# Five modulation pieces put into the state space layer, its preparation reordered in layer 0, x loaded from the scalar queue

## The chip, the cores and the metric

The kernel runs on one core of a Trainium2 chip. The metric is the device time of one execution in microseconds (us). A core has engines that each work through an order of their own: PE (TensorE, the matmuls), DVE (VectorE), ACT (ScalarE), POOL (GpSimd) and SP (SyncE, which here only issues transfers). They wait for each other through semaphores.

## What is computed

The reference takes 256 positions of width 1024 through two blocks. The first has four layers; layer i has a mixer (attention, spatial gating, state space, attention) and a conv-gated feed-forward net (FFN), each behind an RMS norm and with a residual. The second block is modulated: 48 vectors are made from a condition vector by one large product, and scale, shift and gate its norms and residuals. Cut to what the change touches:

```python
def s5_layer(xn, w_in, lam_re, lam_im, log_dt, b_re, b_im, c_re, c_im, d_skip, w_glu):
    u = xn @ w_in
    dt = exp(log_dt); mag = exp(dt * lr)
    ar, ai = mag * cos(dt * li), mag * sin(dt * li)      # the layer's sines
    ...                                                  # bbar from ar, ai, b
    x = associative_scan(a, bbar u)                      # along the 256 positions
    y = c_re x.re - c_im x.im + d_skip * u
    a, g = split(gelu(y) @ w_glu)
    return a * sigmoid(g)

mod   = silu(c)     @ w_mod + b_mod                      # 1024 x 6144, for the second block
mod_c = silu(c_ctx) @ w_mod + b_mod
lb    = cumsum(softmax(lb_tab))[layer]                   # lower bounds of the second block's gates
```

## The kernel before

**Weights.** Everything is fp32 in two parts: each half of a weight tile (128 x 1024) gets a rounded copy `wh` on ACT (L347) and a residual `wl` on DVE (L356), and a product is three matmuls (L488 to L490). `Stream` loads tiles of 1 MB in the order of a plan, through SP's queue, into three raw buffers. The next load is issued when the second half of a tile has been split, or, for a tile that is not split, when its matmuls are done with it.

**Order of work.** The program is written as one sequence; each engine gets its instructions in that order. `tick` counts triple matmuls; `after(n, fn)` puts fn's instructions n ticks later, and `spread` does so for a list of steps with gaps. So numbers in tables (`S5`, `PREP`, the gaps in `s5_prep`) set where steps stand.

**Modulation pieces.** The product with `w_mod` is cut into 24 pieces (`mod_units`). A piece is a unit (16 matmuls at L1447 with 32 columns of stationary data, straight from an unsplit weight tile), a copy `mpart` of its 128 x 256 result on ACT (L1450), and a rest (4 small matmuls at L1455, then two ACT operations at L1460). The step of piece n issues the rest of piece n - 1 and then unit n. The first `S5[1]` = 16 pieces are done in the state space layer (called m2), all of them from its third channel tile (kt = 2) on; the other eight stand in the FFN behind it (f2), one for each of its steps j = 1 to 8.

**State space layer** (`s5`, L1244). Four projections psu2.0 to psu2.3 give u. Each is scaled on DVE (`s5_t`) and copied into the layout of u (`s5_u`, L1339). For each of eight channel tiles kt: `vmm` (tile s5v, L1268), `scan` (six operations on DVE, L1283 to L1285), `scan2` (the recurrence itself, L1293), `back` (L1299 to L1302, tile s5_x), `ymm` (tile s5y, L1310 and L1316) and a gelu on ACT (L1323). scan(kt + 1) stands behind ymm(kt).

**Preparation of that layer.** `s5_prep` issues it in layer 0: p0 to p5 make the coefficients on 128 x 32 tiles (p3 has the exponential and the sines on ACT, L1079, with a load of the sine table and one of the table in use before), then placements of B and C. `place_c` and `lower_bounds` (one small exponential on ACT, `lb_e`, L1483) stood at the end of layer 0's attention.

**Layer 0's attention.** psv, psq, psk are projections, v, q0, qh/ql, k0, kh/kl their evictions; z0.kt are the scores of a pair of heads; ze0, zh0, zl0 the softplus chain; its parts zh0 and zl0 go back to PE for the cumulative sums, which are added into z0.kt.

**Start.** SP issues the vectors, the two halves of x around the halves of the first weight tile, then the rest. ACT squares x for the norm (tile `nsq`, one buffer) and DVE adds the squares up.

Of the kernel before, what the change touches and what calls it, by code (L numbers as in the profile page):

```python
# [9 lines left out]
F32 = mybir.dt.float32  # L10
# [6 lines left out]
P = 128  # L17
L = 256
# [36 lines left out]
PREP = (33, 7)  # L55
MODU = 48
X2 = (16, 56, 69, 11, 106, 29, 18, 31)
LAT = (8, 9, 23, 24, 19, 14)
# [47 lines left out]
LATE = ((), (1, 2))  # L106


S5 = (5, 16, 1, 1, 1, 14, 0, 0, 0, 0)


_VEC = [
# [293 lines left out]
class Kern:  # L406
# [113 lines left out]
    def setup(self, pp):  # L520
# [4 lines left out]
        self.xT = self.apool.tile([P, KT, L], F32, name="xT")  # L525
        load = lambda o, i: nc.sync.dma_start(out=o, in_=i)
        load(self.cols[:, :P], ins["vecs"][:, :P])
        half = lambda q: load(self.xT[:, 4 * q:4 * q + 4, :], ins["x"][:, 4 * q:4 * q + 4, :])
        half(0)
        self.W = Stream(self, ins["weights"], lambda: half(1))  # L530
        self.W._load()
# [63 lines left out]
    def norm_square(self, pr, late=()):  # L595
        nc = self.nc
        x = self.xT[:, 2 * pr:2 * pr + 2, :]
        if pr == 0:
            nc.scalar.activation(self.acc, x, AF.Square)
        else:  # L600
            sq = self.pp.tile([P, 2, L], F32, tag="nsq", bufs=1, name=f"sq_{self.nname}_{pr}")
            nc.scalar.activation(sq, x, AF.Square)
            self.add_later(pr, self.acc, sq, late)

# [442 lines left out]
    def s5_prep(self, sp):  # L1047
# [74 lines left out]
        def p5():  # L1122
# [5 lines left out]
            tt(V, t1, am, lim, ALU.mult)  # L1128
            tt(V, t0, t0, t1, ALU.subtract)
            tt(V, cim, t0, den, ALU.mult)  # L1130
        for p, gap in ((p0, 4), (p1, 4), (p2, 4), (p3, 26), (p4, PREP[1]), (p5, PREP[1])):
            step(p, gap)
        b3 = lambda q: q.unsqueeze(2).to_broadcast([P, 32, 16])
        v3 = lambda q: q.rearrange("p (a b) -> p a b", a=32)
# [14 lines left out]
        def place_c():  # L1149
            for q in range(2):  # L1150
                for g in range(2):
                    act(C[:, 2 + q, :, 16 * g:16 * g + 16], v3(Cc[:, q, :]), AF.Copy,
                        scale=sgn[:, 2 * q + g:2 * q + g + 1])
        step(place_c, 0)
        def place(tp, q, e):
            if e == 0:
                st[q] = tp.tile([P, 32, 2, 2, 16], F32, tag="s5e", name=f"s5_E{q}")
# [26 lines left out]
                    V.tensor_copy(K0[o + 32:o + 64, :, 1, :], di[o + 32:o + 64])  # L1184
        def late(tp):

            h = {}
            for q in range(2):
                j = 4 * q + 1
                h[j, "a"] = [lambda q=q: place(tp, q, 0)]  # L1190
                h[j, "g"] = [lambda q=q: place(tp, q, 1)]
                for g in range(3):
                    h[j + 1, "agd"[g]] = [lambda q=q, g=g: trans(q, g)]
                h[j + 2, "a"] = [lambda q=q: trans(q, 3)]
                h[j + 2, "g"] = [lambda q=q: k0(tp, q)]
            return h
# [1060 lines left out]
    def run(self):  # L2257
# [6 lines left out]
        for i in range(DEPTH):  # L2264
# [3 lines left out]
            if m == 2:  # L2268
                with self.phase(f"p_m{i}") as pp:
                    self.fillers = self.mod_units()  # L2270
                    self.s5(i, pp)
                s5.pop().close()
                s5.pop().close()
                pp = pf.enter_context(self.phase(f"p_f{i}"))
                self.s5_glu(i, nx, pp)
                hooks = {}
            else:
                if i == 0:
                    s5.append(ExitStack())
                    self.table = "natural_log_exp_and_others"  # L2280
                    steps, late = self.s5_prep(s5[0].enter_context(self.phase("p_s50", psum=False)))
                    self.spread(PREP[0], [(fn, min(g, PREP[1]) if n > 5 else g) for n, (fn, g) in enumerate(steps)] + [(self.lower_bounds, 0)])
                if i == 3:
                    cp = pc.enter_context(self.phase("p_ctx", psum=False))
                with self.phase(f"p_m{i}") as pp:
                    (self.attention, self.sgu)[m](i, nx, pp)
                if i == 1:
                    s5.append(ExitStack())
                    sp = s5[1].enter_context(self.phase("p_s51", psum=False))
                pp = pf.enter_context(self.phase(f"p_f{i}"))  # L2290
                hooks = late(pp) if i == 0 else self.s5_tables(sp) if i == 1 else {}
                if i == 1:
                    hooks.setdefault((9, "a"), []).append(self.mod_inputs)
# [92 lines left out]
```

## Time and profile before

| | us |
|---|---|
| median of 3 runs | 1621.68 (1620.92 to 1625.38) |
| profiled execution, its own time | 1621.46 |
| its span | 1619.7 |
| PE busy | 1584.7 (98%) |
| DVE busy | 1257.2 (78%) |
| ACT busy | 994.4 (61%) |
| chain that ended last | PE 84%, DVE 8%, ACT 4% |

The profile is of one execution. Its mean granted clock is 0.993 of full speed. Busy shares are averages over stages with different limits; the waits of single engines, with what ended them, and busy time by stretch tell more. Times within the profile count from the start of the span.

### The profile page before, as it was taken

Reading aid. Unit: us, or ns where it says so; the run is one execution under the profiler, and the core shown is the slowest. Engines: PE = TensorE matmul, PEld = TensorE weight load, DVE = VectorE, ACT = ScalarE, POOL = GpSimd, SP = SyncE. Lnnn points to the kernel's source line nnn. Section 1 sums busy time; section 2 is a strip of 40 time slices with the busy share of each in tenths; the row PEclk is TensorE's granted clock in tenths of the full one; section 3 lists DMA queues with packets and bytes.
Section 4 is the critical chain, followed back from the end, with each engine's and each line's share of the span. In section 5 each row is a group of like instructions: output and inputs, shape, how many; then the busy total and the mean of one; then the engine's idle time right before and its main releaser. Section 6 shows DMA issues by size and latency. Waiting matters only on the chain.

```text
span 1619.7 us, 33776 instructions
## 1 busy us (share of the span) xinstructions
PE 1584.7 (98%) x14370; PEld 1533.2 (95%) x14370; DVE 1257.2 (78%) x1897; ACT 994.4 (61%) x1487; POOL 42.8 (3%) x121
## 2 busy tenths in 40 slices
PE   9899999999999989999999999999999999999997
PEld 8889999999999987799999999999999998899997
DVE  6878877778999889878777765898886697786554
ACT  6776666566778653455556677766566563465443
POOL 0000000010000000000000100000003000000000
PEclk9999999999999999999999999999999999999999
DMA  8424554555455525856666432555545521246551
GB/s 309 139 95 172 194 187 179 200 191 186 170 199 216 195 105 209 321 204 233 233 234 227 187 134 105 209 192 199 197 155 215 204 94 53 104 147 230 187 205 53
DMA packets 42918, 294.27 MB, mean 182 GB/s; under 512 B 4944, under 2 KB 6224, under 8 KB 8336
## 3 DMA queue, kind: packets, MB, share of 16 engines
q1 hardware_dynamic: 41984, 289.04, 49.3%
q0 software_dynamic: 784, 3.08, 0.5%
q8 instruction: 112, 1.84, 0.4%
q14 instruction: 38, 0.31, 0.1%
HBM read 291.06 MB, written 1.05 MB: 180 GB/s over the span
## 4 chain that ended last, share of the span: by engine, by line
PE 84%; DVE 8%; ACT 4%; DMA 1%; issue 1%; POOL 0%; SPq 0%; DVEq 0%; ACTq 0%; POOLq 0%
DVE wl L356 2%; DMA raw<-in_weights_dram 1%; PE mod L1447 1%; PE fb L488 1%; PE fb L490 1%; PE fb L489 1%; PE gug L490 1%; PE gug L488 1%; PE gug L489 1%; ACT wh L347 1%; PE gua L488 1%; PE gua L490 1%; PE gua L489 1%; PE s5y L1316 1%; PE mod L1455 1%
## 5 line engine op out<-in xcount | busy, mean ns | idle before, releaser
L356 DVE TENSOR_TENSOR wl<-raw,wh 128x1024 fp32r<-128x1024 f32 (+1 forms) x496 | 594.2, 1214 | 112.5 <-ACT wh L347 29.1
L347 ACT ACTIVATE wh<-raw 128x1024 fp32r<-128x1024 f32 (+1 forms) x496 | 511.2, 1049 | 199.1 <-DMA raw<-in_weights_dram 42.0
L488 PE MATMUL fb<-gph,wh 128*128 128x256 f32 x176 | 49.0, 278 | 0.2 <-DVE gy L2160 0.2
L490 PE MATMUL fb<-gph,wl 128*128 128x256 f32 x176 | 48.7, 277 | 0.0
L489 PE MATMUL fb<-gpl,wh 128*128 128x256 f32 x176 | 48.6, 276 | 0.0
L490 PE MATMUL gug<-xh_f,wl 128*128 128x256 f32 x144 | 39.9, 277 | 1.2 <-DVE wl L356 1.2
L488 PE MATMUL gug<-xh_f,wh 128*128 128x256 f32 x144 | 39.8, 276 | 0.0
L489 PE MATMUL gug<-xl_f,wh 128*128 128x256 f32 x144 | 39.8, 276 | 0.0
L490 PE MATMUL gua<-xh_f,wl 128*128 128x256 f32 x144 | 39.8, 276 | 0.0
L489 PE MATMUL gua<-xl_f,wh 128*128 128x256 f32 x144 | 39.8, 276 | 0.0
L488 PE MATMUL gua<-xh_f,wh 128*128 128x256 f32 x144 | 39.8, 276 | 0.0
L488 PEld LDWEIGHTS fb<-gph,wh 128*128 128x128 f32 x176 | 33.1, 188 | 0.3 <-DVE gy L2160 0.3
L490 PEld LDWEIGHTS fb<-gph,wl 128*128 128x128 f32 x176 | 33.0, 188 | 0.2 <-DVE wl L356 0.2
L489 PEld LDWEIGHTS fb<-gpl,wh 128*128 128x128 f32 x176 | 33.1, 188 | 0.0
L490 PEld LDWEIGHTS gug<-xh_f,wl 128*128 128x128 f32 x144 | 27.0, 188 | 1.4 <-DVE wl L356 1.4
L488 PEld LDWEIGHTS gug<-xh_f,wh 128*128 128x128 f32 x144 | 27.0, 188 | 0.0
L488 PEld LDWEIGHTS gua<-xh_f,wh 128*128 128x128 f32 x144 | 27.0, 188 | 0.0
L489 PEld LDWEIGHTS gua<-xl_f,wh 128*128 128x128 f32 x144 | 27.0, 188 | 0.0
L490 PEld LDWEIGHTS gua<-xh_f,wl 128*128 128x128 f32 x144 | 27.0, 188 | 0.0
L489 PEld LDWEIGHTS gug<-xl_f,wh 128*128 128x128 f32 x144 | 27.0, 188 | 0.0
L583 ACT ACTIVATE xh_f<-xT,cols 128x256 fp32r<-128x256 f32 x32 | 14.6, 503 | 19.7 <-DVE xT L746 19.7
L1447 PE MATMUL mod<-raw,mod_c 128*32 128x256 f32 x384 | 25.7, 385 | 0.0
(3594 smaller groups left out, 6590.8 us busy)
## 6 DMA issues: line engine op xcount, KB each, us to landing
raw<-in_weights_dram SPq DMA_DIRECT2D x268, 1024.0 KB, 4.9
raw<-in_weights_dram SPq DMA_DIRECT2D x4, 512.0 KB, 5.0
xT<-in_x_dram SPq DMA_DIRECT2D x2, 512.0 KB, 5.6
s_C<-in_s_c_dram SPq DMA_DIRECT2D x1, 1024.0 KB, 5.8
ctx_t<-in_ctx_dram POOLq DMA_DIRECT2D x1, 1024.0 KB, 5.6
out_dram<-out SPq DMA_DIRECT2D x4, 256.0 KB, 2.6
raw<-in_weights_dram SPq DMA_DIRECT2D x1, 768.0 KB, 4.2
s_BT<-in_s_bc_dram SPq DMA_DIRECT2D x1, 512.0 KB, 7.0
```

What stands on the lines that cost most here:

```text
L347: self.k.nc.scalar.activation(self.h[n], r, AF.Copy)
L356: self.k.nc.vector.tensor_tensor(self.l[n], r, self.h[n].bitcast(F32), op=ALU.subtract)
L488: mm(out, lhsT=lh, rhs=rh, start=start, stop=False, skip_group_check=True)
L489: mm(out, lhsT=lh, rhs=rl, start=False, stop=False, skip_group_check=True)
L490: mm(out, lhsT=ll, rhs=rh, start=False, stop=stop, skip_group_check=True)
L583: nc.scalar.activation(h, src, AF.Identity, scale=scale)
L1316: nc.tensor.matmul(out(r, e), lhsT=C[:, 2 * (1 - e) + q, 4 * kt + r, :], rhs=xs[:, q, z, r, e:e + P], start=False, stop=z == 1 and q == 1, ...
L1447: nc.tensor.matmul(ps[r:r + 32, :], lhsT=cp[:, k, :], rhs=w[:, k, :], start=k < 4, stop=k >= 4, skip_group_check=True)
L1455: nc.tensor.matmul(p2[:, 0, 2 * m:2 * m + 2], lhsT=part[:, m * P:m * P + P], rhs=self.con("sel"), start=m == 0, stop=m == 1, skip_group_ch ...
```

## The change

- `S5[1]` goes from 16 to 21, and three zeros of `S5` become 2, 2 and 1: two pieces ahead of vmm(0), two ahead of ymm(0), one ahead of ymm(1), all in the state space layer's start. From kt = 2 on 16 pieces are done as before. f2 does three pieces, from j = 1 on. In the plan of weights five mod tiles move ahead: two behind psu2.1's, three behind psu2.2's tile.
- In `s5_prep` the gaps of p2, p3 and those from p4 on change; `place_c` and `lower_bounds` leave the attention and are issued in f0, from hooks at its first gate and its first up projection.
- The two loads of x are issued by ACT's queue.
- The first norm's `nsq` gets two buffers.

```diff
-PREP = (33, 7)
+PREP = (33, 5)
-S5 = (5, 16, 1, 1, 1, 14, 0, 0, 0, 0)
+S5 = (5, 21, 1, 1, 1, 14, 0, 2, 2, 1)
...
-        half = lambda q: load(self.xT[:, 4 * q:4 * q + 4, :], ins["x"][:, 4 * q:4 * q + 4, :])
+        half = lambda q: nc.scalar.dma_start(out=self.xT[:, 4 * q:4 * q + 4, :], in_=ins["x"][:, 4 * q:4 * q + 4, :])
...
-            sq = self.pp.tile([P, 2, L], F32, tag="nsq", bufs=1, name=f"sq_{self.nname}_{pr}")
+            sq = self.pp.tile([P, 2, L], F32, tag="nsq", bufs=2 if self.nname == "n0" else 1,
+                              name=f"sq_{self.nname}_{pr}")
...
-        for p, gap in ((p0, 4), (p1, 4), (p2, 4), (p3, 26), (p4, PREP[1]), (p5, PREP[1])):
+        for p, gap in ((p0, 4), (p1, 4), (p2, 41), (p3, 12), (p4, PREP[1]), (p5, PREP[1])):
...
-        step(place_c, 0)
...
-            h = {}
+            h = {(0, "a"): [self.lower_bounds], (0, "g"): [place_c]}
...
-                    self.spread(PREP[0], [(fn, min(g, PREP[1]) if n > 5 else g) for n, (fn, g) in enumerate(steps)] + [(self.lower_bounds, 0)])
+                    self.spread(PREP[0], [(fn, min(g, PREP[1]) if n > 5 else g) for n, (fn, g) in enumerate(steps)])
```

ACT in layer 0, before, around the sines (`s5_C`) and the eviction v0 of psv0.2; wh are copies of weight halves:

```order
L347 ACTIVATE wh10_393<-raw5_285 128x1024
L1079 ACTIVATE s5_C_171<-s5_C_171 128x32
L1079 ACT_TABLE_LOAD
L1079 ACTIVATE s5_C_171<-s5_C_171 128x32 x2
L1079 ACTIVATE s5_C_171<-s5_C_171,s5_hpi_175 128x32
L1114 ACT_TABLE_LOAD
L786 ACTIVATE v0_195<-psv0.2_355,rsy_n0_265 128x256 x2
L347 ACTIVATE wh11_443<-raw5_285 128x1024
```

The same engine now; ze0.0 is the first exponential of the scores z0.0:

```order
L347 ACTIVATE wh10_393<-raw5_285 128x1024
L787 ACTIVATE v0_195<-psv0.2_355,rsy_n0_265 128x256 x2
...
L580 ACTIVATE kh0_190<-k0.0_561 128x512
L347 ACTIVATE wh15_566<-raw7_397 128x1024
L1080 ACTIVATE s5_C_171<-s5_C_171 128x32
L1080 ACT_TABLE_LOAD
L1080 ACTIVATE s5_C_171<-s5_C_171 128x32 x2
L1080 ACTIVATE s5_C_171<-s5_C_171,s5_hpi_175 128x32
L1115 ACT_TABLE_LOAD
L347 ACTIVATE wh16_611<-raw8_470 128x1024
L820 ACTIVATE ze0.0_608<-z0.0_599 128x768
```

The sine run moved from ahead of v0.2 to between kh and the first exponential.

ACT at the start of the state space layer, before; rsx_n2 begins the norm's root, s5_u are the copies of u:

```order
L347 ACTIVATE wh192_7253<-raw96_7060 128x1024
L347 ACTIVATE wh193_7255<-raw96_7060 128x1024
L619 ACTIVATE rsx_n2_7312<-pss_n2_7307,eps_101 128x2
L1339 COPY s5_u_7243<-s5_t0_7365 32x2x128 x4
L347 ACTIVATE wh194_7379<-raw97_7123 128x1024
L347 ACTIVATE wh195_7381<-raw97_7123 128x1024
L1368 ACT_TABLE_LOAD
L1339 COPY s5_u_7243<-s5_t1_7440 32x2x128 x8
L1323 ACTIVATE s5_y0_7495<-s5y0_7454 128x2x128
```

The same engine now:

```order
L620 ACTIVATE rsx_n2_7306<-pss_n2_7301,eps_101 128x2
L1339 COPY s5_u_7243<-s5_t0_7359 32x2x128 x4
L1368 ACT_TABLE_LOAD
L1450 COPY mpart0_7381<-mod0_7372 128x256
L1460 ACTIVATE mod_7242<-mod20_7383,cols_84 128x2 x2
L1450 COPY mpart1_7399<-mod1_7390 128x256
L1339 COPY s5_u_7243<-s5_t1_7455 32x2x128 x8
L1460 ACTIVATE mod_7242<-mod21_7469,cols_84 128x2 x2
L1450 COPY mpart2_7485<-mod2_7476 128x256
L1460 ACTIVATE mod_7242<-mod22_7487,cols_84 128x2 x2
L1450 COPY mpart3_7503<-mod3_7494 128x256
L1323 ACTIVATE s5_y0_7546<-s5y0_7505 128x2x128
```

The parts mpart0 to mpart3 came in behind the copies of u, and the four weight copies that stood ahead of s5_y0 now stand behind it, for the tiles raw100 and raw102.

PE at the same place, before, behind the last matmul of psu2.1:

```order
L1268 MATMUL s5v1_7423<-s5_u_7243,s5_BT_172 128x128 x8
L1310 MATMUL s5y0_7454<-s5_u_7243,s5_K0_173 32x128 x8
L1316 MATMUL s5y0_7454<-s5_x_7244,s5_C_171 32x128 x32
L488 MATMUL psu2.2_7507<-xh_n2_7149,wh192_7253 128x256
L489 MATMUL psu2.2_7507<-xl_n2_7150,wh192_7253 128x256
```

and now (mod20 is the rest of piece 0, mod21 of piece 1; ahead of s5v0, where nothing stood, mod0, mod20 and mod1 came in the same way):

```order
L1268 MATMUL s5v1_7438<-s5_u_7243,s5_BT_172 128x128 x8
L1455 MATMUL mod21_7469<-cons_83,mpart1_7399 128x2 x2
L1447 MATMUL mod2_7476<-raw98_7251,mod_c_6773 32x256 x8
L1455 MATMUL mod22_7487<-cons_83,mpart2_7485 128x2 x2
L1447 MATMUL mod3_7494<-raw99_7370,mod_c_6773 32x256 x8
L1310 MATMUL s5y0_7505<-s5_u_7243,s5_K0_173 32x128 x8
L1316 MATMUL s5y0_7505<-s5_x_7244,s5_C_171 32x128 x32
L488 MATMUL psu2.2_7558<-xh_n2_7149,wh192_7559 128x256
```

Two rests and two units moved in between s5v1 and s5y0; the rest of piece 2 needs mpart2.

DVE behind scan(1), before:

```order
L1285 TENSOR_TENSOR s5_w1.1_7498<-s5_w1.1_7498,s5_w3.1_7500 128x512
L356 TENSOR_TENSOR wl195_7508<-raw97_7123,wh195_7381 128x1024
L356 TENSOR_TENSOR wl196_7516<-raw98_7251,wh196_7512 128x1024
L356 TENSOR_TENSOR wl197_7544<-raw98_7251,wh197_7514 128x1024
L1293 SCALAR_TENSOR_TENSOR s5_w0.1_7497<-s5_keep_174,s5_w0.1_7497 128x128 x4
```

and now, with six residuals ahead of scan2(1):

```order
L1285 TENSOR_TENSOR s5_w1.1_7549<-s5_w1.1_7549,s5_w3.1_7551 128x512
L356 TENSOR_TENSOR wl192_7567<-raw100_7388,wh192_7559 128x1024
L356 TENSOR_TENSOR wl193_7569<-raw100_7388,wh193_7561 128x1024
L356 TENSOR_TENSOR wl194_7573<-raw102_7492,wh194_7563 128x1024
L356 TENSOR_TENSOR wl195_7575<-raw102_7492,wh195_7565 128x1024
L356 TENSOR_TENSOR wl196_7609<-raw103_7571,wh196_7603 128x1024
L356 TENSOR_TENSOR wl197_7611<-raw103_7571,wh197_7605 128x1024
L1293 SCALAR_TENSOR_TENSOR s5_w0.1_7548<-s5_keep_174,s5_w0.1_7548 128x128 x4
```

The residuals 192 to 194 moved here from ahead of scan(0), and the load of raw103 is issued behind wl193.

## Rows read from the trace of the kernel before

**Rows 1.** Waits of PE, whole span; in total, times, longest (us).

```profile
engine line waited for: us in total, times, longest us
PE z0.0_612 L798 <- ACT kh L580: 4.5, 1, 4.5
PE z0.7_1273 L798 <- DVE zl0.7_1284 L850: 2.8, 1, 2.8
PE pss_n L1595 <- issue: 1.3, 1, 1.3
```

**Rows 2.** Busy time by stretch; PEclk is the granted clock.

```profile
128.00:300.00 172.00, 172.00 (x1609) 171.66 (x1609) 145.11 (x211) 110.53 (x151) 1.01 (x2) 1.00 0.52 189
690.00:862.00 172.00, 171.89 (x1559) 166.61 (x1559) 134.10 (x190) 101.01 (x151) 0.00 (x0) 1.00 0.62 228
119.90:123.30 3.40, 3.40 (x20) 2.78 (x18) 0.00 (x0) 0.81 (x1) 0.00 (x0) 0.50 0.03 5
590.90:597.70 6.80, 6.58 (x33) 6.38 (x34) 6.30 (x11) 4.66 (x7) 0.00 (x0) 0.50 0.43 154
```

The columns of rows 2: stretch, its length, busy time of PE, PEld, DVE, ACT and POOL (with the number of instructions), PEclk, DMA share, GB/s.

**Rows 3.** SP's queue at the start: start, duration, instruction (timeline).

```profile
1.18 0.42 SPq L526 DMA_DIRECT2D xT<-in_x_dram  x1
```

**Rows 4.** ACT in layer 0, around the sines and kh.

```profile
33.34 0.21 ACT L1079 ACTIVATE s_C<-s_C 128x32 f32<-128x32 f32 x1
...
36.85 0.84 ACT L786 ACTIVATE v<-psv0.2_355,rsy_n 128x256 f32<-128x256 f32 x2
...
47.41 0.63 ACT L580 ACTIVATE kh<-k0.0_578 128x512 fp32r<-128x512 f32 x1 [3.56 <-DVE k0.0_578 L865]
...
50.93 0.81 ACT L819 ACTIVATE ze0.0_621<-z0.0_612 128x768 f32<-128x768 f32 x1 [0.99 <-PE z0.0_612 L798]
```

**Rows 5.** DVE in layer 0: the eight small operations, and zl0.0.

```profile
45.26 1.51 DVE L1078 TENSOR_TENSOR s_C<-s_C 128x32 f32<-128x32 f32 x8
...
58.99 0.95 DVE L850 TENSOR_TENSOR zl0.0_623<-ze0.0_621,zh0.0_622 128x768 fp32r<-128x768 f32 x1
```

**Rows 6.** ACT and DVE at the end of layer 0's attention.

```profile
114.94 2.54 ACT L1079 ACTIVATE s_C<-s_K,cons 128x512 f32<-128x512 f32 x4
118.42 0.95 DVE L850 TENSOR_TENSOR zl0.7_1284<-ze0.7_1282,zh0.7_1283 128x768 fp32r<-128x768 f32 x1
```

**Rows 7.** ACT at the start of the state space layer.

```profile
590.61 1.74 ACT L1339 COPY s_u<-s_t 32x256 f32<-32x256 f32 x4 [5.61 <-DVE s_t L1334]
592.37 2.00 ACT L347 ACTIVATE wh<-raw 128x1024 fp32r<-128x1024 f32 x2
594.39 1.28 ACT L1368 ACT_TABLE_LOAD   x1
601.44 3.53 ACT L1339 COPY s_u<-s_t 32x256 f32<-32x256 f32 x8 [5.76 <-DVE s_t L1334]
605.00 0.41 ACT L1323 ACTIVATE s_y<-s5y 128x256 f32<-128x256 f32 x1
```

**Rows 8.** DVE there: scan(0) begins, three residuals, scan2(1) begins.

```profile
594.60 0.68 DVE L1283 TENSOR_TENSOR s_w0.0_7395<-s5v,s_tab 128x512 f32<-128x512 f32 x1
...
607.51 3.49 DVE L356 TENSOR_TENSOR wl<-raw,wh 128x1024 fp32r<-128x1024 f32 x3
610.92 1.36 DVE L1293 TENSOR_TENSOR_SCAN s_w0.1_7497<-s_keep,s_w0.1_7497 128x128 f32<-128x128 f32 x4
```

**Rows 9.** PE there: s5v0, s5y0 and s5y1.

```profile
591.12 2.92 PE L1268 MATMUL s5v<-s_u,s_BT 64*128 64x128 f32 x16 [1.79 <-ACT s_u L1339]
...
602.06 2.45 PE L1316 MATMUL s5y<-s_x,s_C 128*32 128x128 f32 x64 [2.35 <-DVE s_x L1299]
...
614.78 3.61 PE L1316 MATMUL s5y<-s_x,s_C 128*32 128x128 f32 x64 [2.97 <-DVE s_x L1299]
```

**Rows 10.** PE in f2: rest of one piece, unit of the next.

```profile
758.81 0.51 PE L1455 MATMUL mod<-cons,mpart 128*128 128x2 f32 x4
759.25 1.07 PE L1447 MATMUL mod<-raw,mod_c 128*32 128x256 f32 x16
```

**Rows 11.** The page's list of transfers: KB each, median us from issue to landing.

```profile
raw<-in_weights_dram SPq DMA_DIRECT2D x268, 1024.0 KB, 4.9
```

## The prediction

> **What bounds the kernel now.** I read the waits of TensorE first, then busy time by stretch, then single instructions around each edit. TensorE (PE) is busy 98% of the span, so an edit counts by what it does to PE's order. In the conv FFNs PE never stops: 172.00 of 172.00 us in f0 and 171.89 of 172.00 in f2 [rows 2]. Its larger waits stand where the change works: 4.5 us at z0.0 (first scores of layer 0), 2.8 at z0.7 (last scores), 1.3 at pss_n, and two of 2.35 and 2.97 at the start of the state space layer [rows 1, 9]. After such a wait the granted clock reads 0.50 (the 1.2 GHz level): 119.9 to 123.3, and 590.9 to 597.7 while PE was busy 6.58 of 6.80 us [rows 2]. The sum is made against the profiled run, 1621.46 us (span 1619.7 and 1.8 around it), 0.2 under the median of 1621.68. A measurement of this kernel can tell about 0.3% (4.9 us) from no change.
>
> **f2, three pieces in place of eight.** A piece takes PE from 758.81 (0.51 of rest matmuls) through 759.25 plus 1.07 (the 16 unit matmuls): 1.51 in all [rows 10]. PE is full there, so five fewer are worth 7.5 us; between 1.44 (the next matmul's overlap taken off) and 1.58 each, 7.2 to 7.9. **−7.5.**
>
> **Start.** x's halves leave SP's queue, on which each took about 0.43 to issue ahead of the first weights [rows 3], and a second nsq buffer removes what PE waits for at pss_n, 1.3 [rows 1]. Together 1.8 if both pass to the end; if the transfers fill their engines anyway, only some 0.3. I take two thirds: **−1.2.** ACT issues x, but before its first work, which waits for x: free.
>
> **Layer 0.** Before, the sine run stands on ACT from 33.34 to 36.85, ahead of v0.2's eviction: 3.5 us with its two table loads [rows 4]. Everything behind it is late up to kh at 47.41, hence PE's 4.5. Without it, and without the eight small operations of 1.51 on DVE ahead of k0 [rows 5], kh comes earlier by about what PE waits for it at z0.0, 4.5, and that wait all but goes. But the run is not gone: it now stands between kh and the first exponential. From kh's end (48.04) to 50.93 ACT took 2.9; now two weight copies of 1.0 and the run take 5.5, 2.6 more. And the 1.51 of DVE now stand ahead of zl0.0. So zl0.0, done at 59.94 before [rows 5], comes only 0.4 earlier (−4.5 + 2.6 + 1.5). PE reaches the sums that need it at least 4.5 earlier and waits there for nearly all of that. What is late next is thus zl0.0: this half of the edit brings 0 to −0.5 and perhaps a new slow stretch, up to +2.0 (half of 3.4, and a little).
>
> The end of the layer is different. place_c (2.54 on ACT from 114.94) holds back lb_e's exponential, the lb operations on DVE wait for it, and zl0.7 stands behind them at 118.42 [rows 6]; what it needs of ACT, zh0.7, stands right ahead of place_c. With both gone zl0.7 is done by about 116.1, near where PE asks for it (119.42 − 2.78 = 116.6): 2.8 goes, and with it the stretch at half speed behind it, 3.4 us with PE full, worth half of what work it held, 1.5. Together −4.3. With +0.8 for the middle: **−3.5**, between −4.8 and −2.3.
>
> **f0.** place_c's 2.54, lb_e and two more table loads of 1.28 go to ACT there, and DVE waits once for lb_e. PE is full [rows 2] and weights are split ahead of it; what hides them is ACT's free third of this stretch (110.53 busy of 172). **+0.3**, between 0 and +1.5 (lead lost once, bounded by DVE waiting for one load).
>
> A table load reads 1.28 in the row [rows 7], and the sine run with two of them takes 3.51, in which its four small operations leave no room for more. The Trainium skill (ScalarE: Activation LUTs, What ACT_TABLE_LOAD costs) adds about 1.38 of drain to each switch; by that the state space term below would be 1.4 larger and the whole sum +3.8. The rows speak against it here.
>
> **The state space layer's start: five pieces in.** I follow the order that front shows, each step from rows.
> (a) One weight residual (1.16) leaves the front of the norm's chain; about 0.8 passes, since pss_n's end then decides. So the s_u copies start near 589.8, not 590.61 [rows 7]. ACT: copies 1.74, table load 1.28, then mpart0 (a 128x256 move, 0.41 as s_y): 593.2. PE has finished piece 0's unit at 589.5 and now waits 3.7 for mpart0, ahead of s5v, where before it waited 1.79. What queues behind that wait is piece 1 and s5v, and behind s5v DVE's whole scan. Then rest 0.5, unit 1.0 and s5v: at 2.4 GHz about 1.2, at the low level 2.92 as the row has it [rows 9], rest and unit then about double. scan(0) starts at 596.0 to 598.9; before, 594.60 [rows 8]: +1.4 to +4.3.
> (b) ACT's copies of t1 start 6.84 after scan(0) (601.44 − 594.60) and take 3.53 [rows 7]. Piece 1's result and mpart2 stand behind them, 0.9. So PE waits some 6 us for mpart2; rest 0.5, piece 3's unit 1.0, s5y0 2.45 [rows 9]. s5y0 ends 15.3 after scan(0), 17.6 at half speed; before, 9.9 (604.51).
> (c) ACT makes wh192 only behind s_y0. To scan2(1) then: s_y0 0.41, two copies 2.0, residual 1.16, which frees the buffer for raw103; its megabyte 4.9 [rows 11]; copy 1.0, residuals of 196 and 197 2.3: 11.8. Before it was 6.4 (610.92 − 604.51), the weights being split ahead; DVE now carries six residuals in the place of three [rows 8].
> (d) scan2(1) to s5y1's end: 7.5 before (618.39 − 610.92) with s5y1 at 3.61 in a slow stretch; about 6.1 without one.
> Sum from scan(0): 33.2 to 36.9 against 23.8. With (a): +10.8 to +17.4. Behind s5y1 PE does the same matmuls in the same order as before with as many pieces (16), so nothing gives it back. Taken: both waits drop the clock, but part of each slow stretch lies in idle time: **+14.3.**
>
> **Sum.** −7.5 − 1.2 − 3.5 + 0.3 + 14.3 = +2.4: **1623.9 us.** The pieces cost more in the pauses, which they lengthen, than they cost in f2.
>
> **Rivals.** A, faster: the pauses take the pieces as meant, and the layer's start stays as long as now. −7.5 − 1.2 − 3.5 + 0.3 = −11.9: 1609.6. For it: PE idles 2.35 and 2.97 there anyway and ACT some 5 us before t0. Against: in the order each piece's rest stands on PE ahead of s5v or s5y0, and its mpart on ACT behind copies that DVE releases late. By the page TensorE: Matmul & The Clock Gate (What's actually happening) of the Trainium skill it is activity that lifts the throttle; if the pieces so kept PE at 2.4 GHz, up to 3.4 of the 6.8 us at 0.50 would come back too, and A would give 1606. 0.13.
> B, slower: the half-speed stretch covers all PE work between the first new wait and s5y1. Place: the units, s5v and s5y0; price: the upper ends of (a), (b) and (d), +17.4 in place of 14.3, so 1627.0. It decides from +16.8 on (1626.5 less the other terms). For it: the clock fell at 590.9 after a wait of only 1.79. Against: a new wait of 3.7 to 6 us swallows part of such a stretch. 0.22.
> C: layer 0's edit doesn't do what it says; the z0.0 wait comes back whole at the sums, its slow stretch passes on through the layer, and the end of the layer waits again: term 0, 1627.4. For it: zl0.0 is nearly as late as before. Against: nothing is left ahead of zl0.7. 0.08.
>
> **How the numbers follow.** Forecast 0.57, A 0.13, B 0.22, C 0.08. All low ends together give −3.7, 1617.8; all high ends +9.1, 1630.6. That holds forecast, B and C; the 8 in 10 go from 1617 to 1630. Faster by over 0.3% (under 1616.8): A, 0.13. Slower (over 1626.5): B, C and 0.03 of the forecast's own upper part, 0.33. Within: 0.54.
>
> **What would show it.** After, PE must show waits at a mod rest matmul of about 3.7 and 6 us before s5v0 and s5y0, and scan2(1) some 27 to 29 after scan(0) where it was 16.3. In f2 the five j without a piece must be 1.5 shorter. The z0.0 wait must be gone and one at its sums have come; z0.7's must be gone. I am wrong if the rests don't wait, if wh192 is made before s_y0's gelu in time, or if the megabyte of raw103 was requested earlier than wl193.

## The result and the profile after

The changed kernel takes 1640.91 us (median of 14 runs, 1632.66 to 1649.24), the kernel before on the same chip 1627.4 (14 runs, 1618.87 to 1636.52). The ratio is 1.0079, 95% interval 1.0057 to 1.0101: slower by 0.8%, some 13 us. The forecast was 1623.9, with a range to 1630. The profiled execution took 1634.32, span 1632.5 (before 1621.46 and 1619.7): +12.8 of span, so the trace holds the difference that the medians show.

Waits of PE after the change, whole span (engine, line, releaser: us in total, times, longest):

```profile
PE mod L1455 <- ACT mpart L1450: 10.3, 3, 5.7
PE s5t0.0_2022 L1165 <- ACT s_E L1080: 4.8, 1, 4.8
PE s5y L1316 <- DVE s_x L1299: 2.9, 1, 2.9
PE z0.0_599 L799 <- DVE zl0.0_610 L851: 2.4, 1, 2.4
PE z0.0_599 L799 <- ACT zh0.0_609 L850: 1.8, 1, 1.8
```

Of the old waits [rows 1] those at kh, z0.7 and pss_n are gone. The first line and the last two were forecast. The second was not: `s5t0.0`, a transpose in f0 of the state space layer's B.

**Where the time goes.** PE is nearly always busy, so I follow the start of one instruction on DVE per stage and subtract its start in the kernel before. In the table "f0, start" is the first operation of f0's first gate (150.42 before), "f0, end" that of its last, and so on; scan(0) and scan2(1) are those of the state space layer, "last" is the first output copy. All columns are us against before; e1 to e13 are the experiments below.

| kernel | f0, start | f0, end | f1, end | scan(0) | scan2(1) | f2, start | f2, end | last |
|---|---|---|---|---|---|---|---|---|
| after | −3.8 | +2.4 | +2.4 | +5.7 | +19.1 | +18.4 | +10.8 | +12.8 |
| e1 | −3.8 | +3.7 | +3.7 | +3.7 | +3.7 | +3.5 | +3.5 | +4.6 |
| e2 | −3.4 | −2.8 | +4.9 | +8.3 | +22.2 | +21.9 | +14.1 | +15.9 |
| e3 | −4.1 | −2.5 | +5.2 | +9.6 | +23.5 | +23.6 | +15.8 | +18.6 |
| e4 | −4.3 | +1.2 | +8.9 | +7.8 | +20.8 | +26.5 | +18.5 | +26.6 |
| e5 | −4.6 | +2.3 | +10.0 | +8.9 | +15.9 | +27.1 | +19.3 | +19.4 |
| e6 | −5.4 | +0.1 | +0.1 | −1.6 | +1.8 | +12.5 | +5.1 | +5.6 |
| e7 | −4.1 | −5.0 | −5.0 | −5.0 | −5.0 | −6.9 | −6.9 | −6.9 |
| e8 | −3.9 | −4.9 | −4.8 | −4.8 | −4.8 | −4.5 | −5.3 | −4.6 |
| e9 | −3.1 | −4.1 | −4.0 | −4.0 | −4.0 | −5.1 | −4.9 | −4.7 |
| e10 | −5.2 | −6.1 | +1.6 | +0.5 | +3.9 | +8.7 | +1.0 | +1.3 |
| e11 | −4.3 | −5.3 | −5.3 | −5.3 | −5.3 | −7.1 | −6.7 | −6.1 |
| e12 | −4.2 | −5.2 | +2.5 | +1.4 | +4.8 | +5.9 | −1.7 | −1.7 |
| e13 | −3.3 | −4.3 | +3.4 | +3.9 | +3.9 | +2.8 | +2.6 | +2.6 |

For the changed kernel: start and layer 0 −3.8, f0 +6.2, the layer +15.9, f2 −7.6, what follows +2.0; together +12.8. (The steps of 7.7 in f1 of e2 to e5, e10, e12 and e13 are the slower matmuls of the last section, not an edit: no kernel's code differs there.) Each row is one execution. Kernels with the same code up to a column differ there by up to about 2 us: the changed kernel, e1, e4, e5 and e6 start f0 at −3.8 to −5.4 and lose 5.5 to 7.5 in it, and e7, e8, e10, e12 and e13 start it at −3.3 to −5.2. So a difference of 1 us between two rows means little by itself.

**f0.** ACT after the change, timeline (start, us, instruction, idle time before it and what ended it):

```profile
147.37 1.10 ACT L1007 ACTIVATE fy0.0.0_1693<-fz0.0.0_1691,cols 128x256 f32<-128x256 f32 x2 [1.92 <-DVE fz0.0.0_1691 L1002]
148.48 1.28 ACT L1483 ACT_TABLE_LOAD   x1
149.78 0.22 ACT L1483 ACTIVATE lb_e<-lb_e 128x16 f32<-128x16 f32 x1
...
156.37 1.28 ACT L1015 ACT_TABLE_LOAD   x1 [0.95 <-DVE fy0.0.1_1742 L997]
157.67 0.63 ACT L1015 ACTIVATE fy0.0.1_1742<-fy0.0.1_1742 128x512 f32<-128x512 f32 x1
158.21 2.55 ACT L1080 ACTIVATE s_C<-s_K,cons 128x512 f32<-128x512 f32 x4
...
161.61 1.08 ACT L1007 ACTIVATE fy0.1.0_1815<-fz0.1.0_1813,cols 128x256 f32<-128x256 f32 x2
...
171.15 1.32 ACT L1080 ACTIVATE s_E<-s_BT,cons 128x512 f32<-128x512 f32 x2
```

DVE and PE there:

```profile
162.23 0.48 DVE L997 SCALAR_TENSOR_TENSOR fy0.1.0_1815<-fz0.1.0_1813,cols,fy0.1.0_1815 128x255 f32<-128x255 f32 x1 [3.07 <-ACT fy0.1.0_1815 L1007]
```

```profile
172.52 1.12 PE L1165 MATMUL s5t0.0_2022<-cons,s_E 128*128 128x128 f32 x4 [4.78 <-ACT s_E L1080]
```

ACT and DVE pass each gate of the FFN to and fro: DVE makes fz, ACT scales it (fy), DVE adds the conv's taps, ACT applies the silu, DVE the gate. lb_e with its table load puts 1.5 into that chain and holds up DVE too; the load back and place_c put in 3.8 more, and DVE stands 3.07. The second copy of s_E comes at 171.15. In the kernel before, ACT and PE at the same place were:

```profile
169.34 1.32 ACT L1079 ACTIVATE s_E<-s_BT,cons 128x512 f32<-128x512 f32 x2
```

```profile
172.33 0.60 PE L1165 MATMUL s5t0.0_2022<-cons,s_E 128*128 128x128 f32 x4
```

There s_E was ready at 170.66 and PE asked for it at 172.33, a room of 1.67. Now s_E is ready 1.8 later, PE asks 4.6 earlier (172.52 − 4.78 = 167.74) and stands 4.78. The granted clock reads 0.50 from 170.0 to 176.8; PE works for 4.3 us of that, which costs it some 2 us more (an estimate: half of that time). Against it stands 0.5 to 0.9 that the kernel before had lost up to 172.33 to the slower matmuls of the last section. The sum, 4.8 + 2 less that, is the 6.2 of the table. The clock (window, its length, PE, PEld, DVE, ACT and POOL busy, PEclk, DMA share, GB/s):

```profile
166.00:170.00 4.00, 1.73 (x16) 1.53 (x14) 3.93 (x7) 2.59 (x4) 0.00 (x0) 1.00 0.64 262
170.00:174.00 4.00, 1.48 (x7) 1.48 (x8) 3.06 (x5) 3.39 (x6) 0.00 (x0) 0.50 0.69 244
```

**The state space layer's start.** PE after the change, the pieces and what they stand ahead of:

```profile
591.17 1.07 PE L1447 MATMUL mod<-raw,mod_c 128*32 128x256 f32 x16
595.94 0.61 PE L1455 MATMUL mod<-cons,mpart 128*128 128x2 f32 x4 [3.70 <-ACT mpart L1450]
596.48 1.83 PE L1447 MATMUL mod<-raw,mod_c 128*32 128x256 f32 x16
598.24 2.01 PE L1268 MATMUL s5v<-s_u,s_BT 64*128 64x128 f32 x16
...
611.32 1.01 PE L1455 MATMUL mod<-cons,mpart 128*128 128x2 f32 x4 [5.68 <-ACT mpart L1450]
612.26 1.93 PE L1447 MATMUL mod<-raw,mod_c 128*32 128x256 f32 x16
```

ACT in the same stretch (compare [rows 7]):

```profile
592.52 1.69 ACT L1339 COPY s_u<-s_t 32x256 f32<-32x256 f32 x4 [5.05 <-DVE s_t L1334]
594.22 1.28 ACT L1368 ACT_TABLE_LOAD   x1
595.52 0.37 ACT L1450 COPY mpart<-mod 128x256 f32<-128x256 f32 x1
...
607.15 3.42 ACT L1339 COPY s_u<-s_t 32x256 f32<-32x256 f32 x8 [8.36 <-DVE s_t L1334]
610.59 0.41 ACT L1460 ACTIVATE mod<-mod,cols 128x2 f32<-128x2 f32 x2
610.89 0.37 ACT L1450 COPY mpart<-mod 128x256 f32<-128x256 f32 x1
...
618.11 0.40 ACT L1323 ACTIVATE s_y<-s5y 128x256 f32<-128x256 f32 x1 [3.42 <-PE s5y L1316]
618.39 3.88 ACT L347 ACTIVATE wh<-raw 128x1024 fp32r<-128x1024 f32 x4
626.62 2.01 ACT L347 ACTIVATE wh<-raw 128x1024 fp32r<-128x1024 f32 x2 [4.35 <-DMA raw<-in_weights_dram]
```

And DVE, which ends the same stretch (compare [rows 8]):

```profile
600.30 0.69 DVE L1283 TENSOR_TENSOR s_w0.0_7410<-s5v,s_tab 128x512 f32<-128x512 f32 x1 [6.60 <-PE s5v L1268]
...
627.72 2.36 DVE L356 TENSOR_TENSOR wl<-raw,wh 128x1024 fp32r<-128x1024 f32 x2 [3.62 <-ACT wh L347]
630.00 1.36 DVE L1293 TENSOR_TENSOR_SCAN s_w0.1_7548<-s_keep,s_w0.1_7548 128x128 f32<-128x128 f32 x4
```

mpart stands behind the copies of u and a table load, and PE's rest waits 3.70 and 5.68 for it; the weights' copies stand behind s_y, and scan2(1) behind the weights. From scan(0) to scan2(1) it is 29.7 us, before 16.3.

### The profile page after: what moved, and what is told of

Read it like the earlier page. It is cut to its first block, busy times and chain, and to the rows that moved or that the text cites. A ratio compares the mean times of both kernels' runs of the same rounds, so it can differ in the third digit from the quotient of the medians.

```text
span 1632.5 us, 33765 instructions
## 1 busy us (share of the span) xinstructions
PE 1589.3 (97%) x14370; PEld 1536.9 (94%) x14370; DVE 1257.2 (77%) x1897; ACT 997.5 (61%) x1489; POOL 42.9 (3%) x121
## 4 chain that ended last, share of the span: by engine, by line
PE 87%; DVE 6%; ACT 4%; issue 1%; DMA 1%; POOL 0%; SPq 0%; DVEq 0%; ACTq 0%; POOLq 0%
DVE wl L356 2%; PE mod L1447 1%; PE fb L488 1%; PE fb L490 1%; PE fb L489 1%; PE gug L490 1%; PE gug L488 1%; PE gug L489 1%; PE s5y L1316 1%; ACT wh L347 1%; PE gua L488 1%; PE gua L490 1%; PE gua L489 1%; DMA raw<-in_weights_dram 1%; PE mod L1455 1%
## 5 line engine op out<-in xcount | busy, mean ns | idle before, releaser
L488 PE MATMUL fb<-gph,wh 128*128 128x256 f32 x176 | 49.0, 279 | 0.2 <-DVE gy L2160 0.2
L490 PE MATMUL fb<-gph,wl 128*128 128x256 f32 x176 | 48.8, 277 | 0.0
L490 PE MATMUL gug<-xh_f,wl 128*128 128x256 f32 x144 | 39.9, 277 | 1.2 <-DVE wl L356 1.2
L488 PE MATMUL gug<-xh_f,wh 128*128 128x256 f32 x144 | 39.8, 276 | 0.0
L488 PE MATMUL gua<-xh_f,wh 128*128 128x256 f32 x144 | 39.8, 276 | 0.0
L490 PE MATMUL gua<-xh_f,wl 128*128 128x256 f32 x144 | 39.8, 276 | 0.0
L488 PEld LDWEIGHTS fb<-gph,wh 128*128 128x128 f32 x176 | 33.1, 188 | 0.3 <-DVE gy L2160 0.3
L490 PEld LDWEIGHTS fb<-gph,wl 128*128 128x128 f32 x176 | 33.0, 188 | 0.2 <-DVE wl L356 0.2
L490 PEld LDWEIGHTS gug<-xh_f,wl 128*128 128x128 f32 x144 | 27.0, 188 | 1.4 <-DVE wl L356 1.4
L490 PEld LDWEIGHTS gua<-xh_f,wl 128*128 128x128 f32 x144 | 27.0, 188 | 0.0
L488 PEld LDWEIGHTS gug<-xh_f,wh 128*128 128x128 f32 x144 | 27.0, 188 | 0.0
L488 PEld LDWEIGHTS gua<-xh_f,wh 128*128 128x128 f32 x144 | 27.0, 188 | 0.0
```

The costliest lines, as they stand in the source:

```text
L488: mm(out, lhsT=lh, rhs=rh, start=start, stop=False, skip_group_check=True)
L490: mm(out, lhsT=ll, rhs=rh, start=False, stop=stop, skip_group_check=True)
```

## Experiments

The diffs of e1 to e5 are against the changed kernel, that of e6 against e5, those of e8 to e11 against e7, and that of e12 against e10; line numbers of later kernels are up to four higher. e1 to e4, e5 to e8, e9 to e11, and e12 and e13 share a chip each. e1 to e6 were executed once each, with spans of 1624.3, 1635.6, 1638.3, 1646.3, 1639.1 and 1625.3; the spans expected for e2 to e4 were missed by 6 to 23 us, 7.7 of each by the step in f1, so these runs are read by stage.

**e1: the pieces go back to f2** (against the changed kernel).

```diff
-S5 = (5, 21, 1, 1, 1, 14, 0, 2, 2, 1)
+S5 = (5, 16, 1, 1, 1, 14, 0, 0, 0, 0)
```

> The change without its five pieces (S5 as before; the start, layer 0 and f0 as changed). Theory: the changed kernel's parts add up, -3.8 us at the first FFN step, +6.2 by the fourth (a wait for the placed B tile), then +15.9 in the state space layer and -7.6 in f2. Then this kernel must stand at +2.4 against before from f0 to the end of f2, span about 1622 to 1624, with no wait at a rest matmul and scan2(1) 16.3 after scan(0). Rival: the state space layer is late for another reason than its pieces (an earlier or later start of its weights); then a good part of the +15.9 stays and the span is above 1628.

Span 1624.3. The shift stays +3.7 from f0's end to scan2(1) and +3.5 to f2's end: the layer's +15.9 and f2's −7.6 are the pieces' and nobody else's, +8.3 together. What is left, a loss of 7.5 in f0, is the preparation's, with the same wait as in the changed kernel:

```profile
PE s5t0.0_2022 L1165 <- ACT s_E L1080: 4.8, 1, 4.8
```

**e2: lower_bounds right behind p1, in layer 0; place_c stays in f0** (against the changed kernel).

```diff
-        for p, gap in ((p0, 4), (p1, 4), (p2, 41), (p3, 12), (p4, PREP[1]), (p5, PREP[1])):
+        for p, gap in ((p0, 4), (p1, 0), (self.lower_bounds, 4), (p2, 41), (p3, 12), (p4, PREP[1]), (p5, PREP[1])):
...
-            h = {(0, "a"): [self.lower_bounds], (0, "g"): [place_c]}
+            h = {(0, "g"): [place_c]}
...
```

(Left out: the index from which `spread` shortens the gaps goes from 5 to 6, since the list has one step more.)

> The changed kernel with lower_bounds moved from f0 to layer 0's start, right behind the first exponential, where its table is loaded; f0 so loses two table loads of 1.28 and the lb operations, place_c stays in f0. Theory (chain): in f0 lb with its tables delays ACT and DVE by 2.4 (seen at the scaling of the second up projection) and place_c by 3.2 more, and PE waits for the B tile behind both; then the scaling of the second projection comes 2.4 earlier, PE's wait for s_E falls from 4.8 to about 2.4, and the span by 2.4 to 4 (a half-speed stretch may go): 1628.5 to 1630. Rival (given back): PE reaches the transpose 4.6 earlier than the first FFN steps can deliver whatever stands in them; the wait stays 4.8, the span 1632.

**e3: place_c at the end of the preparation, as before; lower_bounds stays in f0** (against the changed kernel).

```diff
+        step(place_c, 0)
...
-            h = {(0, "a"): [self.lower_bounds], (0, "g"): [place_c]}
+            h = {(0, "a"): [self.lower_bounds]}
```

> The changed kernel with place_c (2.55 on ACT) back at the end of layer 0's preparation, lower_bounds still in f0. Theory (chain): the wait for s_E falls by 3.2, from 4.8 to about 1.6, and the half-speed stretch behind it shrinks or goes; in layer 0 zl0.7 is not held back, as it was lb that held it, so little comes back there. Span 1627.5 to 1629.5. Rival (given back): wait stays 4.8; or place_c costs in layer 0 what it cost in f0: span 1631 to 1633.

The wait of PE at s5t0.0, first in e2, then in e3:

```profile
PE s5t0.0_2022 L1165 <- ACT s_E L1080: 1.1, 1, 1.1
```

```profile
PE s5t0.0_2022 L1166 <- ACT s_E L1080: 2.3, 1, 2.3
```

Through f0 e2 loses 0.5 and e3 1.6, the changed kernel 6.2. So either step alone leaves a small wait (2.4 and 1.6 were expected), behind which the granted clock stays at 1.00 (166 to 176 in both); only both together make the wait of 4.78 and the fall of the clock. In e2 place_c takes its 2.5 on ACT at the same place, without the two table loads and the wait for lb_e, and most of that is covered. In e3 place_c stands in layer 0's attention again and the old wait at z0.7 stays away, so place_c alone does not make it.

**e4: each rest one piece later, two mpart buffers** (against the changed kernel).

```diff
-            part = self.pp.tile([P, 256], F32, tag="mpart", bufs=1, name=f"mpart{n}")
+            part = self.pp.tile([P, 256], F32, tag="mpart", bufs=2, name=f"mpart{n}")
...
-            if todo:
-                todo.pop()()
+            while len(todo) > (1 if n < 5 else 0):
+                todo.pop(0)()
```

> The changed kernel with the rest of each of the first pieces put off by one piece more (a second mpart buffer), so that no rest stands between a unit and the matmuls of the layer while its mpart is still queued on ACT. Theory W (the waits of 3.7 and 5.7 at the rests, with their half-speed stretches, are the larger part): scan(0) starts some 4.5 earlier, s5y0 ends about 10 to 11 after scan(0) in place of 17.7, and of the +15.9 in the layer 3 to 6 stay, which are the late weights (scan2(1) still 11 to 12 after s5y0's end); span 1620 to 1623. Rival L (the late weights, copies behind s_y0 and raw103 behind wl193, decide): waits go but scan2(1) comes no earlier; span above 1628.

The first wait is gone: scan(0) comes 1.1 earlier against f1's end, where it came 3.3 later. The second is not, so the layer still costs 17.6 where 3 to 6 were expected, and the wait has another releaser:

```profile
PE mod L1455 <- ACT mod L1460: 9.4, 2, 5.4
```

Two rests in a row share one PSUM buffer that ACT empties (L1460), and ACT has the eight copies of u in between:

```profile
609.28 3.42 ACT L1339 COPY s_u<-s_t 32x256 f32<-32x256 f32 x8 [5.91 <-DVE s_t L1334]
612.72 0.41 ACT L1460 ACTIVATE mod<-mod,cols 128x2 f32<-128x2 f32 x2
```

**e5: all five rests only in the third channel tile, five mpart buffers** (against the changed kernel).

```diff
-            part = self.pp.tile([P, 256], F32, tag="mpart", bufs=1, name=f"mpart{n}")
+            part = self.pp.tile([P, 256], F32, tag="mpart", bufs=5, name=f"mpart{n}")
...
-            if todo:
-                todo.pop()()
+            while todo and n >= 5:
+                todo.pop(0)()
```

> The changed kernel with the rests of its first five pieces all held back to kt = 2 (five mpart buffers); the five units stay where they are. In e4 the second wait (5.4) stayed because rest 1 needed the PSUM buffer that ACT empties behind the copies of u. Theory W (PE's waits at rests, both behind ACT's queue): no wait at a rest ahead of s5v0 or s5y0; scan(0) some 4.8 earlier against the layer's start than in the changed kernel, s5y0's end 10 to 11 after scan(0) in place of 17.7, scan2(1) still 11 to 12 behind it; the layer's start (s5y1's end) then late by 4 to 6 in place of 16.4, and kt = 2 longer by some 2. Rival L (the late weights are the larger part): scan2(1) moves by less than 5.

**e6: e5, and the weights of psu2.2 copied ahead of t1's copies of u** (against e5).

```diff
         vmm(0)
+        self.W._high(self.W.nh + 1)
         scan(0)
...
+            if kt == 0:
+                self.W._low(self.W.nh - 1)
             ymm(kt)
```

> As e5, and the two weight copies of psu2.2's tile made ahead of ACT's copies of t1, their residuals right behind back(0), so that raw103 is asked for some 6 us earlier. Theory: what is left in e5 is the late weights, 11.8 from s5y0's end to scan2(1) against 6.4 before; here scan2(1) comes 2 to 3 earlier than in e5 and stands 19 to 20 after scan(0) (16.3 before the change). Rival (DVE is full in this stretch whatever the weights do): no earlier than in e5.

Against f1's end scan2(1) stands at +5.9 in e5 and +1.7 in e6; in the changed kernel at +16.6. So the waits at the rests, with what the low clock cost behind them, made 10.7 of that, the late weights 4.3, and 1.7 is left. Both then lose about 11 up to f2, mostly in the third channel tile, where five rests stand in a row behind ACT's copies of t3. e6, waits of PE in the layer:

```profile
PE mod L1458 <- ACT mod L1463: 5.5, 4, 4.0
```

**e7: no pieces, lower_bounds early, place_c as before** (the edits of e1, e2 and e3 together; the sines' place, x on ACT's queue and nsq stay as changed).

> The change without its pieces, with place_c back in layer 0's attention and lower_bounds at layer 0's start (so nothing is added to f0). Theory (chain): without both, PE waits at the transpose for 0 to 0.5 and the gain of the start and of layer 0, 3.8, reaches f1 whole; median 3 to 5 below before. Rival (given back): the wait at the transpose stays 1 to 2.5 with its half-speed stretch and the kernel is within 2 of before.

1615.7 us (4 runs) against 1629.37: ratio 0.9914, 0.9888 to 0.9941. Start and layer 0 keep what they gain, −4.1, f0 loses nothing and the wait at s5t0.0 is gone. (The −0.9 in f0 is the slower matmuls that the kernel before has there.) The moves within layer 0, then, were worth their price; putting place_c and lower_bounds into f0 was not. The profile shows 6.9 of the 13.7 between the medians; e13 comes back to that. What is left in layer 0:

```profile
PE z0.0_609 L799 <- DVE zl0.0_620 L851: 2.4, 1, 2.4
PE z0.0_609 L799 <- ACT zh0.0_619 L850: 1.2, 1, 1.2
```

**e8: e7 with one piece, ahead of ymm(1)** (against e7).

```diff
-S5 = (5, 16, 1, 1, 1, 14, 0, 0, 0, 0)
+S5 = (5, 17, 1, 1, 1, 14, 0, 0, 0, 1)
```

> As e7, with one piece in the state space layer's start: its unit ahead of s5y1, its rest at kt = 2, so that no rest is waited for. Theory: PE idles 2.97 there, so the unit's 1.0 is free and f2 loses 1.5: 1 to 2 below e7. Rival: the piece's tile takes a raw buffer, the load of the tile behind the next waits for the unit, wh198 then holds ACT's queue ahead of the copies of t2, and the layer grows by 3 to 5: 1.5 to 4 above e7.

1621.91 (10 runs), ratio 0.996, 0.9933 to 0.9987. The layer gives +0.3 where e7's gives −1.9, and f2 −0.8. But e8's layer has lost some 1.5 us to the slower matmuls of the last section that e7's has not (172 matmuls from 690 to 710, in e7 179). So a gain from this piece is not shown, nor is a loss; no new wait at a rest came, and the 3 to 5 of the rival did not come.

**e9: e7 with the sines early, in ACT's idle time ahead of v0** (against e7).

```diff
-        for p, gap in ((p0, 4), (p1, 0), (self.lower_bounds, 4), (p2, 41), (p3, 12), (p4, PREP[1]), (p5, PREP[1])):
+        for p, gap in ((p0, 4), (p1, 1), (p2, 1), (p3, 8), (self.lower_bounds, 8), (p4, PREP[1]), (p5, PREP[1])):
```

> The version without new pieces (e7) with one more edit: p2 and p3 of the preparation run early, so that ACT makes the sines in the idle time from about 27 to 32 us in which it waits for the raw tile of the weights, ahead of v0's eviction, and not between kh and the first exponential. Theory: the waits that are left in layer 0, 2.4 and 1.2 us at z0.0's cumulative sums, and the stretch at clock 0.50 behind them come from the sine run's 3.5 us standing ahead of ze0.0; they go, and kh stays early. Then the first FFN starts 3 to 5 us earlier than in e7 and the span is 1808 less than nothing else changed: some 1608 to 1610. Rival: the run delays v0.2 and so kh again, as in the kernel before; the wait then moves back to the first matmul of z0.0 (1 to 4 us) and the gain over e7 is 0 to 1.

(The 1808 in it is a slip; 1608 to 1610 is meant.) The rival came true: kh is late again and PE waits 3.9 for it at the first scores. f0 starts at −3.1 in place of −4.1, which is within what equal kernels differ by. 1621.39 (10 runs), ratio 0.9979, 0.9952 to 1.0006.

```profile
PE z0.0_626 L799 <- ACT kh L580: 3.9, 1, 3.9
```

**e10: e7 with five pieces whose rests are spread over later tiles, six mpart buffers, and e6's weights** (against e7; e6's lines are not shown again).

```diff
-S5 = (5, 16, 1, 1, 1, 14, 0, 0, 0, 0)
+S5 = (5, 21, 1, 1, 1, 14, 0, 2, 2, 1)
...
-            part = self.pp.tile([P, 256], F32, tag="mpart", bufs=1, name=f"mpart{n}")
+            part = self.pp.tile([P, 256], F32, tag="mpart", bufs=6, name=f"mpart{n}")
...
-            if todo:
-                todo.pop()()
+            for q in range(0 if n < 5 else 1 if n < 8 else 2):
+                if len(todo) > (q if n < S5[1] else 0):
+                    todo.pop(0)()
+            while n == S5[1] and todo:
+                todo.pop(0)()
```

> e7 with the five pieces again, but with the rests lagged by five pieces, drained singly and in pairs from the fourth channel tile on, six mpart buffers, the weights wh192 and wh193 copied ahead of t1's copies of u and their residuals behind back(0). Theory: what the pieces cost in the layer's start is not their matmuls but PE's waits at the rests (some 10.7 us) and the late weights (some 4.3); with both taken away scan2(1) stands only about 1.7 us later relative to the layer's start than before, the rests cost 0.5 each later on (2.75), and the FFN behind gives 7.6 back: 3 to 4 us below e7, span about 1609. Rival: the pieces as such cost what they give back; the waits return at the later rests, behind ACT's copies of u or for PSUM buffers, and the span is 1613 or more.

1617.01 (10 runs), ratio 0.9954, 0.9931 to 0.9977. The layer costs +7.1 and f2 gives 7.6 back: even, as the rival had it, and not the 3 to 4 that were expected. Where two rests stand together the second still waits:

```profile
PE mod L1459 <- ACT mod L1464: 3.2, 5, 0.8
```

**e11: e7 with x on SP's queue again** (against e7).

```diff
-        half = lambda q: nc.scalar.dma_start(out=self.xT[:, 4 * q:4 * q + 4, :], in_=ins["x"][:, 4 * q:4 * q + 4, :])
+        half = lambda q: load(self.xT[:, 4 * q:4 * q + 4, :], ins["x"][:, 4 * q:4 * q + 4, :])
```

> e7 with x's two loads issued by the SP queue again, as before; the second nsq buffer stays. Theory: on ACT's queue the halves of x share the transfer engines with the first weight tile, so the first weight copy starts at 7.91 us in place of 7.69 and nothing is gained; with SP the first copy comes 0.2 earlier, pss_n's wait stays away (nsq), and the time is 0.2 to 0.5 below e7. Rival: the issue times of 0.43 each on SP do pass to the first matmul; then 0.4 to 0.9 above e7.

First weight copy on ACT, first in e11, then in e7:

```profile
7.54 1.06 ACT L347 ACTIVATE wh<-raw 128x1024 fp32r<-128x1024 f32 x1 [0.67 <-DMA raw<-in_weights_dram]
```

```profile
7.97 1.06 ACT L347 ACTIVATE wh<-raw 128x1024 fp32r<-128x1024 f32 x1 [1.15 <-DMA raw<-in_weights_dram]
```

The first weights come 0.43 earlier with SP, the norm's end 0.4 later, and f0 starts 0.3 earlier, less than equal kernels differ by: a trade. 1622.12 (10 runs), ratio 0.9988, 0.9957 to 1.0018, which tells neither from e7 on another chip.

**e12: e10 with the second rest behind the unit** (against e10).

```diff
-            for q in range(0 if n < 5 else 1 if n < 8 else 2):
-                if len(todo) > (q if n < S5[1] else 0):
-                    todo.pop(0)()
+            if n > 4 and todo:
+                todo.pop(0)()
...
                 todo.append(unit(n))
+            if n > 7 and len(todo) > 1:
+                todo.pop(0)()
```

> The drained pieces (e10) with the second rest of a step behind its unit and not directly behind the first rest, for the five steps that drain two. Theory: in e10 the second rest waits 0.5 to 0.8 us each time (3.2 in all) for the one PSUM buffer that ACT has to empty, and the unit in between (1.07) covers that; the layer gets some 2.5 to 3 us shorter, so that from its start to the end of the FFN behind it the kernel stands 2 to 3 us better than the version without new pieces. Rival: the time is then taken by the recurrence on DVE, which PE only waits for later; the layer gets less than 1 us shorter, and both versions come out equal within their intervals.

**e13: e7 unchanged, beside e12.**

> The version without new pieces, unchanged (e7), again, next to the drained pieces on one chip. Theory: the local shifts are those of e7 (-4 at the first FFN, -5 in it, -6.9 at the end), and the ratio lies between that of e7 (0.9914) and those of its close relatives (0.9979 and 0.9988); e12 is 2 to 3 us below it. Rival: both come out equal, since the pieces give back in the FFN just what they cost in the layer.

e12: 1619.77 (12 runs), ratio 0.9958, 0.9933 to 0.9982. e13: 1624.18 (12 runs), 0.9975, 0.995 to 1.0. Ten of e12's runs lie below 1621, nine of e13's above 1623. The wait between rests falls from 3.2 to 0.7:

```profile
PE mod L1459 <- ACT mod L1464: 0.7, 1, 0.7
```

From f1's end to f2's end e12 gains 4.2 (layer +3.4, f2 −7.6), and the kernels without new pieces 0.2 to 1.9 (e1, e7, e9, e11, e13). So five pieces are worth 2 to 4 us there, once next to nothing waits for their rests. The layer still grows, as the rival had it in part: PE now waits 5.0 for the recurrence on DVE at s5y1, before 2.97. e12 beats the kernel before by 0.4%, and so the changed kernel too. e7 and e13 are the same kernel on two chips, and their intervals (0.9888 to 0.9941, 0.995 to 1.0) do not meet: e7's 0.9% did not come again, and the shifts, −6.9 and +2.6 at the end, differ by the step of 7.7 and by 1.8 more.

## Why the prediction was wrong

The sum was +2.4 and the profile gives +12.8. Term by term, forecast against measured: start and layer 0 −4.7 and −3.8; f0 +0.3 and +6.2; the layer's start +14.3 and +15.9; f2 −7.5 and −7.6; nothing and +2.0 behind it.

- **f0 is the step that failed**, 5.9 of the 10.4. It took ACT's free third as cover, from a busy share of a stretch [rows 2], and bounded the loss by one wait of DVE for one table load. "PE is full" and "weights are split ahead of it" hold for the matmuls with weights, but not for s5t0.0, whose input s_E comes from ACT behind everything that was put in. In place of +0.3 came a wait of 4.78 at s5t0.0 and some 2 us at the low clock behind it. e2 and e3 show that it takes lb_e's loads and place_c together. The forecast should have looked for PE's work in f0 that waits for ACT and for how much room it had.
- **The layer's start** was right in its mechanism: waits of about 3.7 and 6 were forecast, 3.70 and 5.68 came; scan2(1) 27 to 29 after scan(0), 29.7 came; (b) 15.3 to 17.6, 17.7 came; (c) 11.8, 12.0 came; (d) 6.1 to 7.5, 7.2 came. From scan(0) to s5y1's end that is 36.9, the upper end of 33.2 to 36.9. So the size was taken 1.6 too low within its bounds, since "part of each slow stretch lies in idle time" was hardly so: the rest, the unit and most of s5y0 behind the second wait ran at half speed (unit 1.93 for 1.07), and s5y1 largely too, as rival B had it. e1, e4, e5 and e6 show the parts.
- **f2** was right: −7.6 for five pieces, and again in e10 and e12.
- **Layer 0**: the waits at kh and z0.7 went, and the sums of z0.0 wait 1.8 and 2.4, as forecast, and the granted clock reads 0.50 behind them (58 to 62). **Start**: x on ACT's queue made the first weights later (7.91 for 7.69), so the gain stands only behind pss_n: the norm's end comes 1.7 earlier. Together 0.9 less than forecast.
- **+2.0 behind f2** had no term. 1.5 of it is the granted clock in the second block's attention, which reads 0.50 from 1364.6 to 1368.0 in the changed kernel and 1.00 at the same matmuls in the kernel before, behind a wait of 0.7 in both. First after, then before (columns window, length, PE, PEclk, DMA share, GB/s):

```profile
1364.00:1368.00 4.00, 4.00 (x21) 0.58 0.01 2
```

```profile
1353.00:1357.00 4.00, 4.00 (x32) 1.00 0.01 2
```

  e4 has the same fall at the same matmuls and e2 one 24 us later; e1 and e3 have none, and no kernel's code differs there, so it comes from no edit. What decides it stays open. The rest, and most of what e3 and e4 lose behind f2 (2.8 and 8.1), is stretches of the slower matmuls of the last section.
- **Rival A** was wrong for the order as written, since the rests waited. e12 shows that its idea was sound in part (the layer grows by 3.4, not by 15.9, and f2 gives 7.6), and that the chain, not the matmuls, was most of the price. The Trainium skill (TensorE: Matmul & The Clock Gate, What's actually happening) has activity release the throttle; the granted clock in e12's first window agrees, where the kernel before read 0.50 from 590.9 to 597.7 [rows 2], and the changed kernel, whose pieces waited, reads 0.50 behind both of its waits. First e12 (columns window, length, PE, PEclk, DMA share, GB/s), then the changed kernel behind its second wait (all columns, as in f0):

```profile
588.00:610.00 22.00, 20.27 (x260) 1.00 0.71 255
```

```profile
612.00:616.00 4.00, 4.00 (x53) 2.22 (x56) 1.31 (x3) 0.79 (x3) 0.00 (x0) 0.50 0.16 33
```

In f0 the load at 148.48 begins 0.01 behind the end of the instruction ahead of it, and the next one starts 0.02 behind its own end; the drain that the Trainium skill (ScalarE: Activation LUTs, What ACT_TABLE_LOAD costs) adds to a table switch, about 1.38, does not show there.

## What to carry to other kernels

A free share of an engine covers new work only if nothing that the bounding engine needs stands behind it in that engine's order: before putting work there, list the matmuls whose inputs that engine makes and how early each input is ready. Work for idle time has to be cut so that its own chain never stands ahead of the main chain: issue the matmuls in the pause, and take the results back where all that they need is long done, with buffers for what lies between. Two short matmuls that share one PSUM buffer wait for the engine that empties it; put other work between them.

## What the runs showed of the hardware

At a granted clock of 1.00 the triple matmuls (L488 to L490, 128x128 by 256 columns) follow each other at one of two distances, 0.113 or 0.118 us, each for long stretches with PE busy throughout. Both stand in one execution of the kernel before, here in f0 (columns as in e12's line above):

```profile
150.00:170.00 20.00, 20.00 (x172) 1.00 0.50 166
174.00:194.00 20.00, 20.00 (x179) 1.00 0.57 201
```

Where a stretch ends differs between executions of one kernel. Here is f1 in e7 and then in e13, which are the same kernel:

```profile
470.00:490.00 20.00, 20.00 (x179) 1.00 0.61 215
```

```profile
470.00:490.00 20.00, 20.00 (x173) 1.00 0.55 197
```

(Some records can be missing, but the shift in the table says the same: 7.7 us over f1 and the mixer ahead of it.) In all fifteen profiles the larger distance begins some 20 us behind f0's end, at the short matmuls of the mixer's norm (pss_n, 128x1). In eight it ends about 27 us later, at the matmuls sg of the spatial gating; in the seven with the step of 7.7 it lasts to the next mixer's pss_n, some 260 us in all. What makes it end or go on stays open. The spans of e7 and e13 differ by 9.5 us, most of it this one stretch. Hence the parts are compared here by shifts within a stage and not by the span.
